# The MLPs of a two-layer hybrid block, multiplied by two by two blocks with seven products for eight

## The chip, the cores and the metric

One core of one Trainium2 chip runs the whole kernel. The metric is the device time of one execution in microseconds. Before the change it is 2652.65 us, the median of three runs (2652.08 to 2658.22). The engines are TensorE (PE; its weight loads, PEld, overlap with its matmuls), VectorE (DVE), ScalarE (ACT) and GpSimd (POOL); SyncE (SP) issues most transfers. The profile shows no transfer as an engine's work.

## The reference, cut to what matters

Two layers work on 512 latent tokens and 256 context tokens of width 1024. Each layer has token mixers and then an MLP; only the MLP changes. All is float32.

```
def sq_relu_mlp(h, w1, w2):                      # w1: 1024 x 4096, w2: 4096 x 1024
    return jnp.square(jax.nn.relu(h @ w1)) @ w2
...
    x = x + g1x * yx                              # yx: the token mixers' output
    hx2 = rmsnorm(x, g_mlp[i]) * (1.0 + sc2x) + sh2x
    x = x + g2x * sq_relu_mlp(hx2, w_ff1[i], w_ff2[i])
    if need_ctx:                                  # layer 0 alone
        ctx = ctx + g1c * yc
        hc2 = rmsnorm(ctx, g_mlp[i]) * (1.0 + sc2c) + sh2c
        ctx = ctx + g2c * sq_relu_mlp(hc2, w_ff1[i], w_ff2[i])
```

So the MLP of layer 0 has 768 token columns and that of layer 1 has 512.

## The kernel before

Activations lie transposed, features on partitions and tokens along the free dimension, as eight tiles x[k] of 128 rows. A float32 matrix product is made of three matmuls: each operand is split into a high half (rounded to float32r) and a low half (the rest), and high by high, high by low and low by high are summed in PSUM (`mm_T`, L438). One output tile is a call of `T_tile` (L451): eight weight blocks of 128 x 128, three matmuls each, per segment of at most 512 token columns.

Weights come in pages of 128 x 1024 floats (512 KB) by the class `Stream` (L220 to L273): a load on SP's queue, a high half on POOL or ACT (L246, L244), a low half on DVE (L257). It runs a page ahead. Their order is recorded in a first dry pass over the program.

The MLP (from L1644) goes by four chunks of 1024 inner features. For each chunk, eight tiles of the first matrix (`ff1`): ACT applies relu from PSUM (L1661), POOL squares (L1662), ACT and DVE split the result (L391, L392). Then eight tiles of the second matrix, which DVE multiplies by a gate and adds into x (L1686). The inner layer stays in SBUF. Layer 0's last chunk is split by token groups (L1693 to L1708), so that the next layer's norm can begin early.

Ahead of the MLP the output projection (tile wo) works in two halves of the columns, `grp`, and the norm of each half (`norm_tail`: multiply by the reciprocal root on DVE or POOL, shift on POOL at L531, split) runs as a background generator while PE works on other tiles; the first five ff1 tiles take the first half alone while the norm of the second is made. Background generators advance by one step per `tick()`; `mods_gen` computes the next layer's modulation vectors on DVE during layer 0's MLP (L371, L373).

SBUF pages of 128 x 768 floats come from one pool of 46 (`pg`), PSUM from four banks of one size (`aps`) and two double ones (`dps`). Every engine and queue works in the order of the program.

Of the kernel before, what the change touches and what calls it, by code (L numbers as in the profile page):

```python
# [12 lines left out]
F32 = mybir.dt.float32  # L13
# [8 lines left out]
LAT = 512  # L22
# [14 lines left out]
NPG = 46  # L37
NRAW = 2
PE_COLS = tuple(range(8, 16))
# [104 lines left out]
def kernel(ctx: ExitStack, tc: tile.TileContext, A: dict, order: list, record: bool, tap=None):  # L144
# [37 lines left out]
    SQ1 = None  # L182
    ALT = ("AD", "PD")
    WOR = 1
    FFR = 1
# [34 lines left out]
    class Stream:  # L220
# [5 lines left out]
        def load(self, j):  # L226
            while self.nraw <= j and self.nraw < len(order):
                k = order[self.nraw]
                a, b = _page_shape(k)
                t = wp.tile([128, 1024], F32, tag="wr", bufs=NRAW, name=nm("wr"))[:, :a * b]  # L230
                nc.sync.dma_start(t, A["wst"][woff[k]:woff[k] + 128 * a * b].rearrange("(p n) -> p n", p=128))
                self.raw[self.nraw] = t
                self.nraw += 1

        def split(self, j):
            while self.nsp <= j and self.nsp < len(order):
                self.load(self.nsp)
                t = self.raw.pop(self.nsp)
# [21 lines left out]
        def get(self, key):  # L260
            if record:
                order.append(key)
            assert order[self.nget] == key, (order[self.nget], key)
            self.split(self.nget)
            if self.nsp == self.nget + 1:
                self.flush()
            self.nget += 1
            return self.hl.pop(self.nget - 1)

        def ahead(self):  # L270
# [41 lines left out]
    junk_a = cst.tile([128, 96], BF16, name="junk_a")  # L312
    rope = cst.tile([128, 2, 4, 32], F32, name="rope")
    vec = [cst.tile([128, NV], F32, name=f"vec{i}") for i in range(depth)]
# [4 lines left out]
    o_d = [drp.tile([8, 128, TOK], F32, name=f"o_d{i}") for i in range(depth)]  # L319
    x_d = drp.tile([8, 128, LAT], F32, name="x_d")  # L320

    def spread_c(streams=(0, 1)):
# [237 lines left out]
    def proj_tok(keys_, hi, lo, toks, N):  # L560
# [8 lines left out]
        for key in keys_:  # L569
            wh, wl = W.get(key)  # L570
            nk = _page_shape(key)[0]
            for k in range(nk):
# [11 lines left out]
                tick()  # L584
        return ds_

    def norm_tail(nr, g, w0, wait, gap, engines):
# [333 lines left out]
    for k in range(6, KT):  # L921
        load_cols(k)
    nc.sync.dma_start(rope, A["rope"])
    for i in range(depth):
# [23 lines left out]
    for i in range(depth):  # L948
# [17 lines left out]
        def small_gen():  # L966
            dve.scalar_tensor_tensor(out=gna, in0=vc[:, V_NAQ:V_NAQ + 1], scalar=0.125, in1=vc[:, V_NAK:V_NAK + 1],
                                     op0=ALU.mult, op1=ALU.mult)
            dve.scalar_tensor_tensor(out=gml, in0=vc[:, V_MQN:V_MQN + 1], scalar=1.0 / math.sqrt(96.0),
                                     in1=vc[:, V_MKN:V_MKN + 1], op0=ALU.mult, op1=ALU.mult)  # L970
            for w in range(2):
                t = rg[w]
# [650 lines left out]
        grp = (((0, 0, 256),), ((0, 256, 512),)) if last else even  # L1623
        nrm2 = Norm(i, x, V_GMLP, 32, 24, grp)
        nf = None
        for g, parts in enumerate(grp):
            a, b = parts[0][1], parts[-1][2]
            W.mode = WOM[g]
            bg.rate = WOR
            for m in range(8):  # L1630
                ps = T_tile(("o", i, m), yh, yl, ((a, b),), "wo")
                for s, p0, p1 in parts:
                    dve.scalar_tensor_tensor(out=x[m][:, p0:p1], in0=ps[:, p0 - a:p1 - a], scalar=g1h[:, s, m:m + 1],
                                             in1=x[m][:, p0:p1], op0=ALU.mult, op1=ALU.add)
                nrm2.stat(m, g, SQ0 if g else None)
            if g == 0:
                nf = bg.add(norm_tail(nrm2, 0, *(TL0, TL4)[i]), front=True)
        bg.finish(nf)
# [4 lines left out]

        mark(f"L{i} mlp")  # L1644
        W.defer = DF[5]
        nf = bg.add(norm_tail(nrm2, 1, *(TL1, TL5)[i]), front=True)
# [175 lines left out]
```

## Time and profile before

| what | value |
|---|---|
| median of three runs | 2652.65 us |
| profiled execution | 2651.59 us |
| its span, first to last instruction | 2649.8 us |
| PE, PEld busy | 2486.3 us (94%), 2194.4 us (83%) |
| DVE, ACT, POOL busy | 1614.6 us (61%), 797.6 us (30%), 895.8 us (34%) |
| granted TensorE clock, mean | 0.972 |
| moved to and from HBM | 255.33 MB read, 25.17 MB written |

Busy shares are means over the span. Matmuls are pipelined, so that one matmul's shown length is longer than the step from its start to the next one's; steps are read from a timeline. [...]

### The profile page before, as it was taken

How to read it: one execution, taken by the hardware profiler on the slowest of the kernel's cores; microseconds unless marked ns; L12 is line 12 of the kernel's file. 1: busy time of each engine (PE TensorE's matmuls, PEld its weight loads, DVE VectorE, ACT ScalarE, POOL GpSimd, SP SyncE). 2: the span in 40 equal slices, each digit the busy share in tenths (PEclk: the TensorE clock that was granted, in tenths of full speed). 3: DMA queues.
4: the chain of work that ended last, by engine and by line, in shares of the span. 5: the costliest groups of instructions: out<-in, count | busy, mean ns of one | idle time of the engine just before them, and what ended most of it. 6: DMA issues, size and time to landing. Idle time of an engine off the chain costs nothing.

```text
span 2649.8 us, 38124 instructions
## 1 busy us (share of the span) xinstructions
PE 2486.3 (94%) x14406; PEld 2194.4 (83%) x14406; DVE 1614.6 (61%) x3303; ACT 797.6 (30%) x1945; POOL 895.8 (34%) x822
## 2 busy tenths in 40 slices
PE   6978999999899998999999989899998898899999
PEld 6868889898788898888888877789887787788887
DVE  7878665775785575655452467565655876643343
ACT  2261241425682122010101125433325741201100
POOL 5232122243342355222222352222253534633222
PEclk6999999999899999999999999999999999899999
DMA  6234322332014433334431322322221045333332
GB/s 222 80 108 157 122 91 88 114 115 83 7 57 167 144 112 110 127 110 145 153 139 61 120 96 80 111 98 78 86 95 55 1 154 166 120 118 95 96 96 96
DMA packets 93255, 282.97 MB, mean 107 GB/s; under 512 B 11152, under 2 KB 11920, under 8 KB 93072
## 3 DMA queue, kind: packets, MB, share of 16 engines
q1 hardware_dynamic: 84240, 257.46, 28.9%
q10 hardware_dynamic: 6912, 15.73, 1.6%
q0 software_dynamic: 1920, 7.34, 0.7%
q8 instruction: 114, 1.87, 0.3%
q14 instruction: 69, 0.57, 0.1%
HBM read 255.33 MB, written 25.17 MB: 106 GB/s over the span
## 4 chain that ended last, share of the span: by engine, by line
PE 65%; DVE 19%; ACT 6%; issue 5%; POOL 4%; DMA 1%; SPq 0%; ACTq 0%; DVEq 0%; POOLq 0%
PE f L438 32%; PE gt L1111 7%; PE S L745 4%; PE pt L576 4%; PE pt L577 4%; PE pt L578 4%; DVE wl L257 3%; PE pv L794 3%; PE T L771 2%; PE br L438 2%; PE wo L438 2%; DVE u L1019 1%; DVE junk L371 1%; ACT junk_a L1408 1%; POOL xn L531 1%
## 5 line engine op out<-in xcount | busy, mean ns | idle before, releaser
L246 POOL TENSOR_SCALAR wh<-wr 128x1024 fp32r<-128x1024 f32 (+2 forms) x297 | 335.9, 1133 | 635.8 <-DMA wr<-wst 244.0
L257 DVE TENSOR_TENSOR wl<-wr,wh 128x1024 fp32r<-128x1024 f32 (+1 forms) x286 | 391.2, 1369 | 151.3 <-POOL wh L246 113.3
L438 PE MATMUL f<-h,wh 128*128 128x512 f32 (+2 forms) x808 | 282.8, 350 | 9.8 <-ACT rl L1661 9.1
L438 PE MATMUL f<-l,wh 128*128 128x512 f32 (+2 forms) x808 | 282.3, 349 | 3.2 <-DVE l L392 3.2
L438 PE MATMUL f<-h,wl 128*128 128x512 f32 (+2 forms) x808 | 280.3, 347 | 0.7 <-DVE wl L257 0.7
L438 PE MATMUL f<-uh,wh 128*128 128x512 f32 (+1 forms) x768 | 273.8, 356 | 5.2 <-DVE x L1700 3.5
L438 PE MATMUL f<-ul,wh 128*128 128x512 f32 (+1 forms) x768 | 273.3, 356 | 0.0
L438 PE MATMUL f<-uh,wl 128*128 128x512 f32 (+1 forms) x768 | 272.1, 354 | 0.0
L631 POOL TENSOR_SCALAR P<-P,rl 128x768 f32<-128x768 f32 (+2 forms) x160 | 136.9, 856 | 384.3 <-DVE rl L630 274.8
L1111 PE MATMUL gt<-h,wh 128*128 128x512 f32 (+1 forms) x576 | 220.0, 382 | 6.8 <-POOL wh L246 5.9
L392 DVE TENSOR_TENSOR ul<-rl,uh 128x768 fp32r<-128x768 f32 (+3 forms) x74 | 66.6, 899 | 255.0 <-ACT uh L391 255.0
L577 PE MATMUL pt<-wl,h 128*128 128x256 f32 (+2 forms) x720 | 211.4, 294 | 10.0 <-DVE wl L257 10.0
L1661 ACT ACTIVATE rl<-f 128x768 f32<-128x768 f32 (+3 forms) x74 | 46.7, 632 | 573.7 <-PE f L438 573.7
L576 PE MATMUL pt<-wh,h 128*128 128x256 f32 (+2 forms) x720 | 214.1, 297 | 5.4 <-POOL wh L246 3.3
L1111 PE MATMUL gt<-h,wl 128*128 128x512 f32 (+1 forms) x576 | 207.7, 361 | 8.8 <-DVE wl L257 8.8
L578 PE MATMUL pt<-wh,l 128*128 128x256 f32 (+2 forms) x720 | 211.0, 293 | 0.0
L1111 PE MATMUL gt<-l,wh 128*128 128x512 f32 (+1 forms) x576 | 208.1, 361 | 0.0
L1662 POOL TENSOR_TENSOR rl<-rl 128x768 f32<-128x768 f32 (+3 forms) x74 | 85.8, 1159 | 315.2 <-ACT rl L1661 315.2
L402 DVE TENSOR_TENSOR ptl<-T,pth 128x384 fp32r<-128x384 f32 (+2 forms) x288 | 132.2, 490 | 97.8 <-ACT pth L396 96.3
L438 PEld LDWEIGHTS f<-h,wh 128*128 128x128 f32 x808 | 155.0, 192 | 29.7 <-issue 5.6
L438 PEld LDWEIGHTS f<-l,wh 128*128 128x128 f32 x808 | 154.8, 192 | 21.5 <-DVE l L392 4.4
L438 PEld LDWEIGHTS f<-h,wl 128*128 128x128 f32 x808 | 154.3, 191 | 18.7 <-DVE wl L257 1.1
(279 smaller groups left out, 6235.3 us busy)
## 6 DMA issues: line engine op xcount, KB each, us to landing
wr<-wst SPq DMA_DIRECT2D x298, 512.0 KB, 3.5
mod<-wmod SPq DMA_DIRECT2D x108, 384.0 KB, 4.3
bias<-bias SPq DMA_DIRECT2D x32, 320.0 KB, 3.6
th_d<-th ACTq DMA_DIRECT2D x24, 384.0 KB, 2.4
thr<-th_d SPq DMA_DIRECT2D x24, 384.0 KB, 3.5
x<-x SPq DMA_DIRECT2D x16, 384.0 KB, 4.9
th_d<-th ACTq DMA_DIRECT2D x24, 256.0 KB, 2.0
thr<-th_d SPq DMA_DIRECT2D x24, 256.0 KB, 3.8
```

Source lines behind the costliest of these rows:

```text
L246: pool.tensor_scalar(hi, t, 1.0, 0.0, op0=ALU.mult, op1=ALU.add)
L257: eng.tensor_tensor(out=lo, in0=t, in1=hi, op=ALU.subtract)
L402: dve.tensor_tensor(out=lo, in0=ps, in1=hi, op=ALU.subtract)
L438: pe.matmul(ps[:, c:c + b - a], wt[:, k, :], mv[k][:, a:b], start=k == 0 and wt is wh and mv is hi, stop=k == kts - 1 and wt is wl)
L576: pe.matmul(o, hi[kk][:, c], wh[:, k, :], start=kk == 0, stop=False)
L577: pe.matmul(o, hi[kk][:, c], wl[:, k, :], start=False, stop=False)
L578: pe.matmul(o, lo[kk][:, c], wh[:, k, :], start=False, stop=kk == total - 1)
L631: pool.tensor_scalar(self.P[:, :w], self.P[:, :w], rl, 1.0, op0=ALU.mult, op1=ALU.mult)
L745: pe.matmul(S[:, c:c + ww], a[r0:r1, qc], b[r0:r1, k0:k0 + ww], start=i_ == 0, stop=i_ == 2)
L794: pe.matmul(o[:, a:b], v_block(V, t, h), mv, start=i_ == 0, stop=i_ == len(ops) - 1, skip_group_check=True)
L1111: pe.matmul(ps[:, :b - a], wt[:, k, :], mv[k][:, a:b], start=k == 0 and wt is wh and mv is hi, stop=k == KT - 1 and wt is wl)
L1662: pool.tensor_tensor(out=t[:, a:b], in0=t[:, a:b], in1=t[:, a:b], op=ALU.mult)
```

## The change

The whole MLP of layer 1, and that of layer 0 but for the second matrix of its last chunk (the plain part), is made by two by two blocks with seven products. A pair `p` is two weight pages, which hold a 2 x 2 arrangement of 512-row by 128-column blocks; the tokens fall in two halves of n columns, 384 in layer 0 and 256 in layer 1. Sums of weight blocks (s1 to s4) and of activation blocks ("1" to "4") are formed ahead; seven products of four k blocks and three matmuls each (84 matmuls a pair) land in three PSUM banks, and sums of these give the four output blocks. There are 16 pairs of the first matrix, all of them first; their outputs, relu and square done, go to DRAM (`u_d`), as three pages X, Y, Z that hold six of the blocks and differences of blocks. Then 12 (layer 0) or 16 (layer 1) pairs of the second matrix read them back, each block once for four pairs, and split them.

`BlockWeights` has its own loads, into three raw buffers in place of two, and its splits run five products ahead. `block_tail` takes the place of `norm_tail` and makes the combined activation blocks. The weight stream of the rest of the kernel is emptied before and after (`bar`). The table of rotary angles moves from a fixed tile to a load in each layer.

```
+    BLEAD = (5, 5)
+    BAHEAD = 5
+    BLOAD, BSPLIT = 6, 3
...
+                for q in (6, 5, 7, 3, 4) if p < BLEAD[i] else (1, 3, 6, 5, 7, 2, 4):
+                    if q != 3:
+                        seq.append((p, q))
+                    elif prev is not None:
+                        seq.append((prev, 3))
...
+    BLOCKS = {1: ("w11", "11"), 2: ("w12", "21"), 3: ("s4", "22"), 4: ("w22", "4"), 5: ("s1", "1"), 6: ("s2", "2"), 7: ("s3", "3")}
...
+        def sums(self, j):
+            if j < len(self.seq) and self.seq[j][1] == 6:
+                p = self.seq[j][0]
+                w11, w21, w22 = self.half(p, 0, 0), self.half(p, 1, 0), self.half(p, 1, 1)
+                pool.tensor_tensor(out=w11, in0=w11, in1=w21, op=ALU.subtract)
+                s2 = self.f[p, "s2"] = pg("s2")[:, :512]
+                pool.tensor_tensor(out=s2, in0=w22, in1=w11, op=ALU.subtract)
+                pool.tensor_tensor(out=w21, in0=w21, in1=w22, op=ALU.add)
+        def split(self, j):
...
+            if q == 6:
+                s4 = self.f[p, "s4"] = pg("s4")[:, :512]
+                pool.tensor_tensor(out=s4, in0=self.half(p, 0, 1), in1=src, op=ALU.subtract)
+            t = self.t[p, name] = wp.tile([128, 1024], F32R, tag="wh", bufs=8, name=nm(name))
+            split_block(t, 512, src)
...
+    def split_block(t, n, src, eng=dve):
+        act.activation(t[:, :n], src, AF.Copy)
+        eng.tensor_tensor(out=t[:, n:2 * n], in0=src, in1=t[:, :n], op=ALU.subtract)
+    def block_tail(nr, g, O, hf, n, w0, wait, gap, engines):
...
+                for eng, o, p, q in ((pool, b3, b22, b12), (dve, b12, b12, b11), (dve, b2, b22, b12), (pool, b21, b21, b2)):
+                    eng.tensor_tensor(out=o, in0=p, in1=q, op=ALU.subtract)
+                yield
+                for j, (name, src, eng) in enumerate((("2", b2, dve), ("1", b12, dve), ("3", b3, pool), ("4", b21, pool), ("22", b22, dve))):
+                    O[name][kk] = pg("h" + name, F32R)
+                    split_block(O[name][kk], n, src, eng)
...
+            dmul = lambda t: pool.tensor_tensor(out=t, in0=t, in1=t, op=ALU.mult)
+            def square(j, t, relu=True):
+                if relu:
+                    later(j + 1, lambda: act.activation(t, t, AF.Relu))
+                later(j + 1, lambda: dmul(t))
+            def add(out, ps, t):
+                dve.tensor_tensor(out=out, in0=ps[:, :n], in1=t, op=ALU.add)
+            def store(p):
+                for slot, k in enumerate("XYZ"):
+                    if k in S[p]:
+                        act.dma_start(u_d[i][p, slot][:, :2 * n], S[p][k][:, :2 * n])
...
+                elif q == 3:
+                    X, Y = st["X"], st["Y"]
+                    add(Y[:, h0], st.pop("c"), Y[:, h0])
+                    square(j, Y[:, h0])
+                    def sums():
+                        Z = st["Z"] = pg("bz")
+                        for o, a, b in ((Z[:, h1], Y[:, h1], Y[:, h0]), (Y[:, h0], Y[:, h0], X[:, h0]), (Z[:, h0], Y[:, h1], Y[:, h0])):
+                            pool.tensor_tensor(out=o, in0=a, in1=b, op=ALU.subtract)
+                    if last or p < 12:
+                        later(j + 1, sums)
+                    later(j + 4, lambda: store(p))
...
+                elif q == 7:
+                    Y = st["Y"]
...
+                        act.activation(Y[:, h1], st["b"][:, :n], AF.Copy)
+                    add(Y[:, h1], st["c"], Y[:, h1])
+                    square(j, Y[:, h1])
...
+            def xadd(m, h, src):
+                for s, a, b in grp[h]:
+                    dve.scalar_tensor_tensor(out=x[m][:, a:b], in0=src[:, a - h * n:b - h * n], scalar=mods[i][:, s, 40 + m:41 + m],
+                                             in1=x[m][:, a:b], op0=ALU.mult, op1=ALU.add)
+            def evac2(j, p, q):
+                st = S.setdefault(p, {})
+                c, m = divmod(p - 16, 4)
+                if q == 1:
+                    st["X"], st["Y"] = pg("bx"), pg("by")
+                    act.activation(st["X"][:, :n], st["b"][:, :n], AF.Copy)
+                elif q == 2:
+                    add(st["X"][:, :n], st.pop("a"), st["X"][:, :n])
+                    xadd(m, 0, st["X"][:, :n])
+                elif q == 6:
+                    act.activation(st["X"][:, n:2 * n], st["b"][:, :n], AF.Copy)
+                elif q == 7:
+                    Y = st["Y"][:, :n]
+                    act.activation(Y, st["b"][:, :n], AF.Copy)
+                    add(Y, st["c"], Y)
+                    xadd(m + 4, 1, Y)
+                elif q == 4:
+                    xadd(m + 4, 0, st.pop("b"))
...
+                elif q == 3:
+                    X = st["X"][:, n:2 * n]
+                    add(X, st.pop("c"), X)
+                    xadd(m, 1, X)
...
+            def plain_split():
+                k = plain[1]
+                if k < 8:
+                    plain[1] += 1
+                    uh[k], ul[k] = pg("uh", F32R), pg("ul", F32R)
+                    t = uf.pop(k)[:, :nq]
+                    act.activation(uh[k][:, :nq], t, AF.Copy)
+                    (pool if k % 2 else dve).tensor_tensor(out=ul[k][:, :nq], in0=t, in1=uh[k][:, :nq], op=ALU.subtract)
+            for j, (p, q) in enumerate(seq):
+                for f in todo.pop(j, ()):
+                    f()
...
+                if not last and j == nlead + 5 * BLEAD[i] + 4:
+                    spread_c()
+                    mgen = mbg.add(mods_gen(i + 1))
+                    mbg.rate = 0.3
+                BW.ahead(j + BAHEAD)
+                for o, name in loads.get(j, ()):
+                    for nme in ("21", "2") if name == "4" else (name,):
+                        for k in range(4):
+                            if k % 2 == 0:
+                                t = pg("uf")
+                            v = t[:, n * (k % 2):n * (k % 2) + n]
+                            slot, h = U_AT[nme]
+                            nc.sync.dma_start(v, u_d[i][4 * (o - 1) + k, slot][:, n * h:n * h + n])
+                            uf.setdefault((o, name), []).append(v)
...
+                for o, name in splits.get(j, ()):
+                    vs = uf.pop((o, name))
+                    if name == "4":
+                        for k in range(4):
+                            pool.tensor_tensor(out=vs[k], in0=vs[k], in1=vs[4 + k], op=ALU.subtract)
+                    for k in range(4):
+                        O[o][name][k] = pg("u" + name, F32R)
+                        split_block(O[o][name][k], n, vs[k], pool)
...
+                for k in range(4):
+                    for i_, (w0, b0) in enumerate(((0, 0), (0, n), (512, 0))):
+                        pe.matmul(ps, wt[:, w0 + 128 * k:w0 + 128 * k + 128], B[k][:, b0:b0 + n],
+                                  start=fresh and k == 0 and i_ == 0, stop=k == 3 and i_ == 2, skip_group_check=True)
+                    if k % 2:
+                        tick()
+                (evac1 if p < 16 else evac2)(j, p, q)
```

## Rows read from the trace of the kernel before

**Rows 1.** The page's chain that ended last, share of the span by line.
```profile
PE f L438 32%; PE gt L1111 7%; PE S L745 4%; PE pt L576 4%; PE pt L577 4%; PE pt L578 4%; DVE wl L257 3%; PE pv L794 3%; PE T L771 2%; PE br L438 2%; PE wo L438 2%; DVE u L1019 1%; DVE junk L371 1%; ACT junk_a L1408 1%; POOL xn L531 1%
```
**Rows 2.** Busy times by stretch, MLPs of layer 0, then of layer 1.
```profile
core 0: us, PE busy (x) PEld busy (x) DVE busy (x) ACT busy (x) POOL busy (x), PEclk, DMA share, GB/s
981.70:1470.90 489.20, 479.09 (x2735) 424.14 (x2736) 245.83 (x486) 61.68 (x90) 137.05 (x119) 1.00 0.34 119
1134.90:1202.10 67.20, 67.20 (x386) 58.98 (x385) 38.04 (x86) 11.61 (x14) 17.38 (x14) 1.00 0.30 104
...
2283.00:2645.70 362.70, 355.66 (x1667) 298.88 (x1666) 151.05 (x167) 44.41 (x84) 121.75 (x113) 0.99 0.32 102
2384.40:2427.90 43.50, 43.50 (x193) 36.03 (x192) 15.84 (x16) 8.61 (x14) 14.44 (x14) 1.00 0.28 86
```
**Rows 3.** Timeline of PE, 959.7 to 966: start, length, engine, line, operation, tiles, form.
```profile
959.86 0.33 PE L438 MATMUL wo<-yh,wh 128*128 128x384 f32 x1
...
965.93 0.33 PE L438 MATMUL wo<-yh,wl 128*128 128x384 f32 x1
```
**Rows 4.** Timeline of PE in layer 1's MLP, 2287 to 2290.
```profile
2287.49 0.28 PE L438 MATMUL f<-l,wh 128*128 128x256 f32 x1
...
2289.89 0.28 PE L438 MATMUL f<-h,wh 128*128 128x256 f32 x1
```
**Rows 5.** POOL by line and form: count, busy us, mean ns, idle before.
```profile
L1586 POOL TENSOR_TENSOR y<-y,thr 128x512 f32<-128x512 f32 x8 | 10.2, 1294 | 13.4 <-DVE thr L1584 13.4
...
L477 POOL TENSOR_TENSOR sq<-sq,sq 128x256 f32<-128x256 f32 x9 | 6.7, 740 | 12.0 <-ACT sq L471 9.2 <-DMA wr<-wst 2.6
...
L257 POOL TENSOR_TENSOR wl<-wr,wh 128x384 fp32r<-128x384 f32 x4 | 4.1, 1028 | 0.3
```
**Rows 6.** Timeline of POOL, 1017 to 1024.
```profile
1017.49 0.83 POOL L1662 TENSOR_TENSOR rl<-rl 128x384 f32<-128x384 f32 x1
1018.29 1.05 POOL L246 TENSOR_SCALAR wh<-wr 128x1024 fp32r<-128x1024 f32 x1
...
1021.35 2.02 POOL L246 TENSOR_SCALAR wh<-wr 128x1024 fp32r<-128x1024 f32 x1
```
**Rows 7.** Timeline of POOL, 2318 to 2328.
```profile
2322.87 0.62 POOL L1662 TENSOR_TENSOR rl<-rl 128x256 f32<-128x256 f32 x1
```
**Rows 8.** DVE by line and form, as in rows 5.
```profile
L1633 DVE SCALAR_TENSOR_TENSOR x<-wo,g1h,x 128x256 f32<-128x256 f32 x24 | 11.4, 475 | 0.7 <-PE wo L438 0.7
...
L392 DVE TENSOR_TENSOR yl<-y,yh 128x512 fp32r<-128x512 f32 x8 | 5.5, 693 | 6.1 <-ACT yh L391 6.1
...
L1633 DVE SCALAR_TENSOR_TENSOR x<-wo,g1h,x 128x384 f32<-128x384 f32 x8 | 4.9, 612 | 4.2 <-PE wo L438 4.0
...
L1633 DVE SCALAR_TENSOR_TENSOR x<-wo,g1h,x 128x128 f32<-128x128 f32 x8 | 2.7, 341 | 1.4 <-PE wo L438 1.4
```
**Rows 9.** Three single lines of DVE: duration in ns as least/median/most, first and last start.
```profile
L371 DVE SCALAR_TENSOR_TENSOR junk<-mod,sB x132: 934/951/2596, 97.4 to 1379.7; 128x768 bf16<-128x768 f32 x132
...
L373 DVE SCALAR_TENSOR_TENSOR junk<-mod,sB x132: 424/425/2318, 98.4 to 1380.7; 128x256 bf16<-128x256 f32 x132
...
L1686 DVE SCALAR_TENSOR_TENSOR x<-f,mods,x x80: 473/749/751, 1076.3 to 2645.7; 128x512 f32<-128x512 f32 x56, 128x256 f32<-128x256 f32 x24
```
**Rows 10.** Timeline of DVE, 1020 to 1026, beside rows 6.
```profile
1020.61 1.84 DVE L257 TENSOR_TENSOR wl<-wr,wh 128x1024 fp32r<-128x1024 f32 x1
1022.38 1.39 DVE L392 TENSOR_TENSOR ul<-rl,uh 128x384 fp32r<-128x384 f32 x1
...
1025.46 0.54 DVE L392 TENSOR_TENSOR ul<-rl,uh 128x384 fp32r<-128x384 f32 x1
```
**Rows 11.** Timelines of DVE and of POOL, 188 to 196.
```profile
189.01 7.33 DVE L257 TENSOR_TENSOR wl<-wr,wh 128x1024 fp32r<-128x1024 f32 x1 [1.99 <-POOL wh L246]
...
189.95 5.31 POOL L1062 TENSOR_TENSOR rg<-rg,u 128x768 f32<-128x768 f32 x3
```
**Rows 12.** Busy times by stretch, the start of the kernel, columns as in rows 2.
```profile
0.00:30.00 30.00, 18.39 (x85) 17.02 (x85) 14.83 (x36) 11.27 (x16) 2.53 (x5) 0.73 0.93 348
...
30.00:60.00 30.00, 20.76 (x99) 18.57 (x99) 28.00 (x50) 4.76 (x6) 26.21 (x14) 0.61 0.39 142
```

More of the change, by code (lines that the diff above doesn't have):

```diff
@@ L268, in get, with bar @@
             return self.hl.pop(self.nget - 1)
+        def bar(self):
+            self.flush()
+            if record:
+                order.append(BAR)
+            assert order[self.nget] == BAR and self.nsp == self.nraw == self.nget
+            self.nget = self.nsp = self.nraw = self.nget + 1
         def ahead(self):
@@ L320 @@
     x_d = drp.tile([8, 128, LAT], F32, name="x_d")
+    u_d = [drp.tile([16, 3, 128, TOK], F32, name=f"u_d{i}") for i in range(depth)]
     def spread_c(streams=(0, 1)):
@@ L1624, with bkeys @@
         nrm2 = Norm(i, x, V_GMLP, 32, 24, grp)
+        if BLK[i]:
+            n = nq // 2
+            pairs = list(range(16 + 4 * (4 if last else 3)))
+            oset = lambda p: 0 if p < 16 else 1 + (p - 16) // 4
+            O = [{name: [None] * 4 for name in U_AT} for _ in range(5)]
+            hf = {}
+            def bkeys(p):
+                if p < 16:
+                    m = 8 * (p // 4) + p % 4
+                    return ("ff1", i, m), ("ff1", i, m + 4)
+                c, m = divmod(p - 16, 4)
+                return ("ff2", i, c, m), ("ff2", i, c, m + 4)
+            seq, prev = [], None
+            for p in range(BLEAD[i]):
+                seq += [(p, 1), (p - 1, 2)] if p else [(p, 1)]
+            seq.append((BLEAD[i] - 1, 2))
+            for p in pairs:
+                for q in (6, 5, 7, 3, 4) if p < BLEAD[i] else (1, 3, 6, 5, 7, 2, 4):
[3 more added lines that the diff above has]
+                        seq.append((prev, 3))
+                prev = p
+            seq.append((prev, 3))
         nf = None
@@ L1635 @@
                 nrm2.stat(m, g, SQ0 if g else None)
+                if BLK[i] and g and m >= 6:
+                    if m == 6:
+                        BW = BlockWeights(seq, [bkeys(p) for p in range(len(pairs))])
+                        BW.load()
+                    else:
+                        W.bar()
+                        BW.ahead(1)
             if g == 0:
-                nf = bg.add(norm_tail(nrm2, 0, *(TL0, TL4)[i]), front=True)
+                nf = bg.add(block_tail(nrm2, 0, O[0], hf, n, *TB0) if BLK[i] else norm_tail(nrm2, 0, *(TL0, TL4)[i]), front=True)
         bg.finish(nf)
```

214 lines of the change are left out of this document (211 added, 3 removed).

## The prediction

> **What bounds the kernel now.** I read the chain of waits first: the reader is to see that the MLP's matmuls (tile f) alone hold 32% of it, and that no other line comes near [rows 1]. Then the busy times by stretch: in layer 0 the MLP part that the change replaces runs from 981.7 to 1470.9 (489.2 us) and an inner chunk of eight tiles takes 67.2 us with PE busy throughout, DVE 38.0 and POOL 17.4; in layer 1 it runs from 2283.0 to 2645.7 (362.7 us), a chunk takes 43.5 us, DVE 15.8 and POOL 14.4 [rows 2]. So PE sets the pace, and everything else hides. A "pair" below is two such tiles, the unit of the change: 16.8 us in layer 0 (67.2/4), 10.88 in layer 1. What the parts before and after the chunks cost beyond that (981.7 to 1470.9 less 28 pairs: 18.8 us; layer 1, less 32 pairs: 14.4) is the norm's serial stretch; I leave it as it is.
>
> **PE's share of the change.** A pair becomes 7 products of 12 matmuls, 84, with 384 columns in layer 0 and 256 in layer 1. 384 columns follow one another every 0.1734 us (36 matmuls, 6.07 us over 35 steps) [rows 3], 256 every 0.120 (21 matmuls, 2.40 over 20) [rows 4]: 14.57 us a pair for 16.8, and 10.08 for 10.88. The second gain is small because a matmul of 256 columns takes more than half of one of 512 (43.5/192 = 0.227 us [rows 2]). Over 28 and 32 pairs PE saves 62.4 + 25.6 = 88 us. That is all the change can give.
>
> **What DVE and POOL get in its place.** Per pair, in the code of the change: POOL forms three weight sums and one more in the split (four operations of 512 columns with two different inputs, 1.294 us each [rows 5]); DVE makes seven low halves of 512 columns (0.693 [rows 8]); ACT makes the high halves. For the first product matrix POOL also squares four blocks and forms three differences for the stored page; for the second, POOL makes seven low halves of activations and one difference, and DVE adds into x, three times from SBUF. POOL with two inputs takes 1.028 us for 384 columns and 0.740 for 256 [rows 5]; squaring (one input twice) 0.83 and 0.62 [rows 6, 7]; DVE's add into x 0.475 for 256 columns, 0.612 for 384, 0.341 for 128 [rows 8].
> Layer 0, first matrix: POOL 5.18 + 3.32 + 3.08 = 11.58, DVE 4.85. Second: POOL 5.18 + 8 x 1.028 = 13.40, DVE 4.85 + 0.612 + 2 x (0.341 + 0.475) = 7.09.
> Layer 1, first: POOL 5.18 + 2.48 + 2.22 = 9.88, DVE 4.85. Second: POOL 5.18 + 5.92 = 11.10, DVE 4.85 + 3 x 0.475 = 6.28.
> Each engine by itself stays near PE's time. They are not by themselves. At 1020.61 DVE starts an operation with two SBUF inputs; POOL's next one, which takes 1.05 us when free, starts at 1021.35 and lasts 2.02, ending 0.92 us after DVE's end; DVE's next, 0.54 us when free, starts at 1022.38 and lasts 1.39, ending 0.40 after POOL's end [rows 6, 10]. Each waits for the whole of the other but for about 0.14 us. At 189.01 one DVE low half lasted 7.33 us behind three POOL operations in a row [rows 11]. DVE reading PSUM doesn't wait: 80 adds, 473 to 751 ns at the most, with POOL at work [rows 9]. So the two times add: 16.43 and 20.49 us a pair in layer 0, 14.73 and 17.38 in layer 1, each above its PE time, and all but the first above the pair of before.
> Layer 0: 16 x 16.43 - 4 x 3.08 (four pairs store no third page) + 12 x 20.49 = 496.5. The modulation vectors of the next layer run here as before, 66 steps of 0.951 + 0.425 us with two SBUF inputs [rows 9]: 90.8, hidden until now. The norm's second half now builds the combined blocks: for each of four k, two differences and two low halves on POOL (4 x 1.028), two differences and three low halves on DVE (5 x 0.54 [rows 10]), 4 x 6.81 = 27.2, less the 8 low halves of before (4.3): 22.9. The plain last chunk splits eight pages read back, on both engines in turn, an estimate of 12.6 from two operations of 384 each. Sum 622.8, and 18.8 of serial stretch: 641.6 against 489.2, +152.4.
> Layer 1: 16 x 14.73 + 16 x 17.38 = 513.8, the norm's extra 17.5 by the 256-column rows, 14.4: 545.7 against 362.7, +183.0.
> Together +335. Against it stands the 0.14 us at each hand-over. DVE's operations of this kind number 408 in layer 0 and 292 in layer 1; if each stands between two POOL operations, 700 x 0.28 = 196 us come back: +139. If they come in runs, as at 189, nearly nothing does. Both patterns stand in the trace; POOL's sums come in threes and its low halves in fours, DVE's splits one at a time, so I take half: **+237**.
>
> [...]
>
> **What else is added, and what hides it.** ACT: 7 high halves of 512 columns and 7 to 10 smaller copies a pair; before, it took 0.83 us for 768 columns (11.61/14) and 0.62 for 512 (8.61/14) [rows 2], so 14.1 and 10.5 us at the most, near PE's time and below the shared sum. Its stores wait for POOL's differences, and the high halves of later weights queue behind them; while POOL has work given to it earlier this costs nothing, and if not, up to one pair's lag at a time. The read-backs go through SP's queue behind weight loads that wait for one of three buffers; they are issued six products ahead, 12 us at the new pace. Traffic grows by about 69 MB (44 pages of 0.39 MB and 48 of 0.26 written, and 96 and 128 blocks of half a page read back, with 16 for the plain chunk); the thickest stretch, layer 1's second matrix, asks 34 MB in at least 174 us, 193 GB/s, where the start of the kernel moved 348 [rows 12]. The empty weight queue at each change of streams: 0 to 5 us, four times, under PE's last wo tiles; taken as nothing. The rope load per layer: nothing, one small load.
>
> **The sum.** The profiled execution took 2651.6 us, span 2649.8 and 1.8 around it; the runs' median is 2652.7, so the two agree. 2651.6 + 237 = 2889, forecast **2890 us**; full credit 2791, none 2987.
>
> **Rivals.**
> *No credit at all*, 2987: runs on POOL as at 189 keep DVE out each time. For it: the code gives POOL up to eight operations at once. Against: rows 6 and 10 show strict turns. 0.15.
> *The clock falls as well*, 3030. PE would idle 30% of the time. [...] Against: the grant was 1.00 and 0.99 over the MLPs of before, short idle times and all (10 and 7 us) [rows 2]. 0.15.
> *POOL alone counts*, 2616, faster: the waiting above belongs to those shapes, and 512-column halves pass beside POOL. Then layer 0 is PE's (-62.4), layer 1's first matrix too (-12.8), its second POOL's (+3.5), and POOL's part of the norm's extra and the plain chunk costs 36. It decides if DVE's low halves last under 0.8 us beside a busy POOL. Rows 6, 10 and 11 speak against it. 0.06.
> *PE stays the bound*, 2564, all 88 us. It needs the same, and the tails hidden. 0.03.
> *The round trip through DRAM or the pages run short*, over 3050: ACT's stores wait for POOL, pages come free late, and both engines idle together. Nothing in the rows gives a price but the lag of one pair (15 to 20 us) now and then; ten of them would do. 0.06.
> The forecast has the rest, 0.55.
>
> **Numbers.** The range runs from 2775 (just under full credit) to 3050 (the clock case inside); outside are the two fast cases and the last. Anything beyond 0.3% (8 us) can be told from no change here: faster 0.09, same 0.01, slower 0.90.
>
> **What would show it.** A chunk of four pairs of layer 1's first matrix lasting 50 to 60 us, not 40; DVE's 512-column low halves at 1.0 us or more in the mean against 0.693, POOL's sums over 1.5 against 1.294; PE's idle time ended by low halves and sums; POOL busy 90% in the MLP. The prediction is wrong if these operations keep their free durations with both engines busy, or if PE is gapless and a chunk takes 40 us (14.57 x 4 = 58 in layer 0).

## The result, and the profile after

The changed kernel takes **3048.99 us** (median of 4, 3047.27 to 3049.47) beside 2652.36 (2649.88 to 2658.22): ratio 1.149, interval 1.147 to 1.151. The forecast was 2890, the range 2775 to 3050; the direction came out, the size lies 1 us inside the upper end of the range.

The profiled execution took 3047.3 us, span 3045.5, 395.7 more than before. First the chain by line, the answer to [rows 1]:

```profile
PE 39%; DVE 21%; POOL 16%; issue 10%; ACT 8%; DMA 5%; SPq 0%; ACTq 0%; POOLq 0%; DVEq 0%
PE gt L1259 7%; PE S L891 4%; PE pt L595 3%; PE pt L596 3%; PE pt L597 3%; POOL u L682 3%; PE br L457 3%; PE pv L940 2%; POOL wr L648 2%; DVE wl L268 2%; PE fb L2011 2%; PE T L917 2%; POOL s L650 2%; DMA wr<-wst 2%; PE lu L457 2%
```

The MLP's matmuls, 32% of it before, are down to 2% for their largest group (fb, line 2011). PE's share fell from 65% to 39%, POOL's rose from 4% to 16%; its low halves of u and its weight sums (lines 682, 648, 650) are now among the named lines. The stretches, columns as in [rows 2] (PEclk, the granted clock, is a share of the full one; it stood at 0.50 from 2510.3 to 2543.3); of each layer the whole block part, its lead (the first four pairs' worth of products), and four pairs inside (28 products), twice for layer 1's first matrix; the last is one of layer 1's second matrix:

```profile
core 0: us, PE busy (x) PEld busy (x) DVE busy (x) ACT busy (x) POOL busy (x), PEclk, DMA share, GB/s
987.00:1654.20 667.20, 489.09 (x2399) 456.27 (x2400) 435.43 (x692) 222.61 (x450) 424.25 (x352) 0.86 0.41 145
987.00:1120.40 133.40, 75.69 (x350) 70.42 (x351) 58.65 (x87) 35.84 (x72) 79.71 (x77) 0.76 0.19 69
1205.60:1291.00 85.40, 69.47 (x337) 66.71 (x336) 59.02 (x99) 26.45 (x54) 51.40 (x44) 0.88 0.39 142
2480.30:3041.30 561.00, 400.79 (x2698) 377.96 (x2698) 273.33 (x429) 215.64 (x506) 394.94 (x397) 0.84 0.35 117
2480.30:2591.00 110.70, 58.02 (x346) 54.38 (x347) 47.12 (x86) 31.19 (x72) 63.69 (x69) 0.71 0.24 76
2591.00:2652.20 61.20, 46.17 (x339) 44.87 (x338) 28.23 (x44) 23.84 (x54) 47.70 (x48) 0.92 0.37 125
2652.20:2710.80 58.60, 46.79 (x339) 45.98 (x338) 27.34 (x40) 23.52 (x54) 43.17 (x44) 0.88 0.36 126
2845.00:2912.40 67.40, 50.82 (x338) 46.46 (x337) 36.54 (x57) 28.27 (x68) 49.67 (x49) 0.87 0.40 126
```

Layer 0's blocks take 667.2 us for 489.2, layer 1's 561.0 for 362.7: +178.0 and +198.3. The rest: 5.3 ahead of layer 0's blocks (987.0 for 981.7) and 14.0 between the two block parts (826.1 for 812.1, the plain chunk among them). Four inner pairs of layer 1's first matrix, 43.5 us before, take 61.2 and 58.6; and no engine is full in the second of these: PE 46.8, POOL 43.2, DVE 27.3. That alone doesn't tell a chain from engines that take turns, for POOL's and DVE's busy times, their waits inside, add up to 70.5. But the trace shows a chain. A lap of it, start, length, engine, operation and line:

```profile
2651.46 0.62 ACT s L681
2652.07 0.28 ACT bx L1891
...
2652.42 0.85 POOL bx L1842
2653.27 1.97 issue
2655.28 0.63 POOL by L1842
...
2655.97 1.08 POOL bz L1901
...
2657.12 1.07 POOL by L1901
...
2658.28 0.73 POOL bz L1901
2659.01 1.23 POOL wr L648
...
2660.32 1.27 POOL s L650
2661.61 0.34 ACT s L681
2661.98 0.45 ACTq L1856
2662.43 0.09 ACT by L1884
...
2662.57 2.94 PE fb L2011 x12
2665.53 0.42 DVE bx L1851
...
2666.30 0.61 ACT s L681
```

The last row is the first again, 14.84 us later (the next two laps take 15.53 and 14.85): one pair, one lap. A product ends, DVE adds it from PSUM, ACT takes the high half of a later weight and, behind it, a relu from PSUM (line 1891), POOL squares two blocks, forms the three differences of the stored page and only then, in the order of its queue, the sums of a weight block that is needed several products later. ACT's high half waits for that sum, and behind it in ACT's queue stand a store (line 1856) and the copy that frees the bank (line 1884), for which the array waits. So work for later products stands ahead of what the current one needs, in two queues. The waits from 2591 to 2774, three such stretches (engine and line, what it waited for, us, times, longest), name the same places:

```profile
ACT s L681 <- POOL s L650: 60.1, 12, 5.1
...
PE fb L2011 <- ACT by L1884: 35.0, 11, 4.3
```

The forecast had priced the two engines' shared access. It is in the trace too: the low halves of the weights on DVE, and two of POOL's sums (least, median and most in ns, first and last start):

```profile
L682 DVE TENSOR_TENSOR w<-wr,w x180: 676/692/1492, 986.9 to 3032.2; 128x512 fp32r<-128x512 f32 x180
L682 DVE TENSOR_TENSOR s<-s,s x120: 676/1076/1759, 1010.9 to 3033.7; 128x512 fp32r<-128x512 f32 x120
L682 DVE TENSOR_TENSOR s<-wr,s x120: 674/896/1773, 1014.6 to 3030.2; 128x512 fp32r<-128x512 f32 x120
...
L650 POOL TENSOR_TENSOR s<-wr,wr x60: 1261/1262/2033, 1008.9 to 3024.4; 128x512 f32<-128x512 f32 x60
...
L662 POOL TENSOR_TENSOR s<-wr,s x60: 1262/1730/1763, 1012.7 to 3026.8; 128x512 f32<-128x512 f32 x60
...
L1851 DVE TENSOR_TENSOR by<-fc,by x92: 409/425/558, 1066.8 to 3037.4; 128x256 f32<-128x256 f32 x48, 128x384 f32<-128x384 f32 x44
```

Free, a low half takes 0.68 us; 130 of the 420 take over 1. The adds that read PSUM don't wait: 0.41 to 0.56 us at the most, by their two widths. So there were two theories for the experiments: **A**, the engines take turns and their work adds up; **B**, the closed chain through the queues.

### The profile page after: what moved, and what is told of

Its sections match the earlier page's. It is cut to its first block, busy times and chain, and to the rows that moved or that the text cites. A ratio compares the mean times of both kernels' runs of the same rounds, so it can differ in the third digit from the quotient of the medians.

```text
span 3045.5 us, 42328 instructions
## 1 busy us (share of the span) xinstructions
PE 2543.5 (84%) x15102; PEld 2305.8 (76%) x15102; DVE 1945.8 (64%) x3797; ACT 1131.0 (37%) x2731; POOL 1443.3 (47%) x1338
## 3 DMA queue, kind: packets, MB, share of 16 engines
q8 instruction: 119, 1.95, 0.3%
## 4 chain that ended last, share of the span: by engine, by line
PE 39%; DVE 21%; POOL 16%; issue 10%; ACT 8%; DMA 5%; SPq 0%; ACTq 0%; POOLq 0%; DVEq 0%
PE gt L1259 7%; PE S L891 4%; PE pt L595 3%; PE pt L596 3%; PE pt L597 3%; POOL u L682 3%; PE br L457 3%; PE pv L940 2%; POOL wr L648 2%; DVE wl L268 2%; PE fb L2011 2%; PE T L917 2%; POOL s L650 2%; DMA wr<-wst 2%; PE lu L457 2%
## 5 line engine op out<-in xcount | busy, mean ns | idle before, releaser
L257 POOL TENSOR_SCALAR wh<-wr 128x1024 fp32r<-128x1024 f32 (+4 forms) x169 | 181.5, 1078 | 364.0 <-PE pt L596 85.6
L268 DVE TENSOR_TENSOR wl<-wr,wh 128x1024 fp32r<-128x1024 f32 (+1 forms) x156 | 227.8, 1464 | 136.7 <-POOL wh L257 99.9
L2011 PE MATMUL fb<-h,w 128*128 128x384 f32 (+1 forms) x888 | 177.9, 368 | 91.5 <-ACT by L1884 60.5
L2011 PEld LDWEIGHTS fb<-h,w 128*128 128x128 f32 x888 | 166.7, 240 | 100.6 <-ACT by L1884 65.9
L2011 PE MATMUL fb<-h,s 128*128 128x384 f32 (+1 forms) x768 | 141.8, 335 | 98.0 <-ACT h L681 45.7
L2011 PE MATMUL fb<-u,w 128*128 128x256 f32 (+1 forms) x672 | 132.5, 363 | 95.6 <-ACT by L1925 92.1
L2011 PEld LDWEIGHTS fb<-h,s 128*128 128x128 f32 x768 | 125.5, 206 | 108.7 <-ACT h L681 47.9
L682 POOL TENSOR_TENSOR u<-uf,u 128x256 fp32r<-128x256 f32 (+1 forms) x196 | 204.2, 1076 | 0.1
L682 DVE TENSOR_TENSOR w<-wr,w 128x512 fp32r<-128x512 f32 x180 | 141.4, 801 | 66.8 <-ACT w L681 65.3
L390 DVE SCALAR_TENSOR_TENSOR junk<-mod,sB 128x768 bf16<-128x768 f32 x132 | 157.8, 1196 | 23.0 <-DMA mod<-wmod 22.3
```

The source lines that it names most:

```text
L257: pool.tensor_scalar(hi, t, 1.0, 0.0, op0=ALU.mult, op1=ALU.add)
L268: eng.tensor_tensor(out=lo, in0=t, in1=hi, op=ALU.subtract)
L390: dve.scalar_tensor_tensor(out=junk, in0=t, scalar=1.0, in1=sB[s], op0=ALU.mult, op1=ALU.mult, accum_out=acc[:, s, j, 0:1])
L682: eng.tensor_tensor(out=t[:, n:2 * n], in0=src, in1=t[:, :n], op=ALU.subtract)
L2011: pe.matmul(ps, wt[:, w0 + 128 * k:w0 + 128 * k + 128], B[k][:, b0:b0 + n], start=fresh and k == 0 and i_ == 0, stop=k == 3 and i_ == 2, s ...
```

## The experiments

**One-input low halves.** DVE copies the high half into the place of the low one, so one of the two SBUF inputs goes.

```
-            split_block(t, 512, src)
+            act.activation(t[:, :512], src, AF.Copy)
+            dve.tensor_scalar(t[:, 512:1024], t[:, :512], 1.0, 0.0, op0=ALU.mult, op1=ALU.add)
```

> The seven low halves of a pair's weights on DVE read one SBUF input in place of two: the high half alone is copied to the low half's place, 512 columns, as many DVE operations as before (so the low parts of the weights are wrong). POOL, ACT, PE, the transfers and the order stay. Theory A (DVE operations with two SBUF inputs and POOL's operations exclude each other, and their sum is the pair's time): 4.85 us a pair leave the sum; layer 1's inner pairs go from 15.3 and 16.8 us to 10 to 11 and 12.5 to 13, layer 0's from 21 and 24 to 16 and 20: 230 to 290 us less, 2760 to 2820 us. Theory B (the pair's time is a closed loop through the queues: POOL's squares, differences and weight sums, ACT's split of a sum and the copy from PSUM behind it, a product, DVE's add, relu, and POOL again): the loop keeps its members and only POOL's waiting inside them goes, 1.3 to 2.6 us a pair: about 110 us less, 2920 to 2950 us.

2925.19 us, ratio 1.103 (1.101 to 1.105): 124 less, inside B's window and above A's. But A's premise was wrong: one input doesn't free this operation from the turns. DVE, then POOL, in the same microseconds:

```profile
2842.15 1.52 DVE L665 TENSOR_SCALAR w<-w 128x512 fp32r<-128x512 f32 x1
2843.59 2.96 DVE L665 TENSOR_SCALAR s<-s 128x512 fp32r<-128x512 f32 x2
...
2847.31 0.42 DVE L665 TENSOR_SCALAR s<-s 128x512 fp32r<-128x512 f32 x1
```

```profile
2842.02 1.35 POOL L650 TENSOR_TENSOR s<-wr,wr 128x512 f32<-128x512 f32 x1
2843.34 1.47 POOL L651 TENSOR_TENSOR wr<-wr 128x512 f32<-128x512 f32 x1
2844.78 1.48 POOL L662 TENSOR_TENSOR s<-wr,s 128x512 f32<-128x512 f32 x1
```

Alone the copy takes 0.42 us (2847.31); beside POOL it lasts 1.52, until the sum has ended and 0.30 beyond (2843.67 against 2843.37), and the next two end 0.29 beyond the third sum (2846.55 against 2846.26). In turns of 0.42 us in place of 0.69, A gives 1.9 us a pair or 115 less, as near to 124 as B's 110; so this run doesn't tell the two apart.

**Differences two products later.** Order alone: the differences and the stores move behind later weights' sums.

```
-                        later(j + 1, sums)
-                    later(j + 4, lambda: store(p))
+                        later(j + 3, sums)
+                    later(j + 6, lambda: store(p))
```

> The three differences for the stored page are put into the program two products later, behind the next pair's three weight sums on POOL, and the stores two products later with them. Same operations, same shared time. Theory A: no change, 3035 to 3065 us. Theory B: three operations, 2.9 us, leave the loop of each pair of the first matrix: 28 pairs x 1.5 to 2.9 us = 40 to 80 us less, 2970 to 3010 us.

3020.86, ratio 1.139 (1.138 to 1.141): 28 less, between the two windows: more than A gives and less than B expected.

**Weights first.** The weights' preparation is issued ahead of the delayed squares and differences, one product earlier.

```
-    BAHEAD = 5
+    BAHEAD = 6
...
             for j, (p, q) in enumerate(seq):
+                BW.ahead(j + BAHEAD)
                 for f in todo.pop(j, ()):
...
-                BW.ahead(j + BAHEAD)
```

> The weight sums and splits run six products ahead in place of five and stand before the squares and differences of the same step in the program. Same operations, same shared time. Theory A: no change, 3035 to 3065 us. Theory B: the square and the three differences of a pair leave the way to the next pair's sums, and the second matrix gets one product more of lead: 60 to 120 us less, 2930 to 2990 us.

2977.43, ratio 1.123 (1.121 to 1.124): 72 less with not one operation fewer, inside B's window; A alone gives nothing here. The edit changes the order in the queues and starts the preparation a product earlier, and no run parts the two.

**Squares on ACT.** All squares of the first matrix leave POOL, 2.48 us a pair in layer 1.

```
-            dmul = lambda t: pool.tensor_tensor(out=t, in0=t, in1=t, op=ALU.mult)
+            dmul = lambda t: act.activation(t, t, AF.Square)
```

> The four squares of a pair of the first matrix go from POOL to ACT (its Square, in place, behind the relu). Theory A: 3.32 us a pair leave the sum in layer 0 and 2.48 in layer 1, 16 pairs each: 93 us less, 2945 to 2970 us. Theory B: POOL no longer waits for ACT's relu before the weight sums, and two squares, 1.5 us, and two hand-overs of some 0.3 us go out of the loop; ACT gets 1.7 to 2.1 us a pair, beside: 50 to 110 us less, 2940 to 3000 us. It does not tell the two apart by its time; by them the first matrix's chunks in layer 1 go from 61 us to 51 or to 53 to 57.

3055.82, ratio 1.153 (1.151 to 1.154): 7 more, where both theories expected less. Four pairs of layer 1's first matrix in this run:

```profile
2655.80:2718.80 63.00, 47.85 (x337) 45.41 (x337) 27.20 (x40) 31.30 (x74) 33.15 (x28) 0.91 0.34 117
```

POOL fell from 43.2 to 33.2 us and the stretch grew by 4.4. This refutes A as the whole account: the sum of the two engines' work went down and the time did not. Nor did B's windows, for time or stretch, come out. The chain of this run says why: the squares only changed the queue they stand in. Its lap, 15.7 us (2655.73 to 2671.41), runs through ACT (relu, square, high halves) and back to POOL's differences and sums, and over these four pairs and the four before POOL waits 57.2 us for ACT's squares.

**Both of the first and third edit together.**

> The two edits that each took time away, together: the low halves of the weights by a one-input copy on DVE (the low parts of these weights are wrong in this run; it shows time only) and the weights' preparation issued ahead of a product's delayed work instead of behind it. Alone they were worth 124 us (2925) and 72 us (2977). If they shorten different things (the load on the two engines' shared access, and the order in the queues), they add: 2835 to 2870. If both only shorten one closed chain of waits, the second finds the chain already cut by the first and something else late: 2890 to 2925. Below 2830 neither picture would hold.

2853.38, ratio 1.075 (1.073 to 1.077): 195.6 less, for 124 + 72 = 196. They add, so neither edit takes the other's gain, as the expectation asked of two separate costs.

**Three weight sums left out.**

```
-                pool.tensor_tensor(out=w11, in0=w11, in1=w21, op=ALU.subtract)
-                s2 = self.f[p, "s2"] = pg("s2")[:, :512]
-                pool.tensor_tensor(out=s2, in0=w22, in1=w11, op=ALU.subtract)
-                pool.tensor_tensor(out=w21, in0=w21, in1=w22, op=ALU.add)
+                self.f[p, "s2"] = w22
```

> Three of the four weight sums per pair left out on POOL (one raw block stands in for the third; the output is wrong, it shows time only). They take about 0.9 to 1.36 us each in the changed kernel's trace, some 3.2 us per pair, 60 pairs: 190 us of POOL's time. Shared access sets the time (theory A): the whole of it comes off, and somewhat more where DVE no longer waits, 2810 to 2870. Closed chain (theory B), in which only two of the three sums stand between a store and the next weights: 60 x 2 us = 120, 2900 to 2950. If neither sets the time but the half-clock stretches of the array do: within 30 us of 3049.

2865.52, ratio 1.080 (1.078 to 1.083): 183 less. The three take 3 x 1.27 = 3.8 us a pair, 229 over 60 pairs: 80% of POOL's time for them stood in the end time, 3.1 us a pair. Both theories have them on the path. The size lies in A's window, which was priced from 190 us; from 229, 183 is 46 short of all three, and from B's two sums, 152, it is 31 more. It decides little.

**Weights first, and the four sums on DVE.** The edit of weights first, and:

```
-                pool.tensor_tensor(out=w11, in0=w11, in1=w21, op=ALU.subtract)
+                dve.tensor_tensor(out=w11, in0=w11, in1=w21, op=ALU.subtract)
...
-                pool.tensor_tensor(out=s2, in0=w22, in1=w11, op=ALU.subtract)
-                pool.tensor_tensor(out=w21, in0=w21, in1=w22, op=ALU.add)
+                dve.tensor_tensor(out=s2, in0=w22, in1=w11, op=ALU.subtract)
+                dve.tensor_tensor(out=w21, in0=w21, in1=w22, op=ALU.add)
...
-                pool.tensor_tensor(out=s4, in0=self.half(p, 0, 1), in1=src, op=ALU.subtract)
+                dve.tensor_tensor(out=s4, in0=self.half(p, 0, 1), in1=src, op=ALU.subtract)
```

> Weights' preparation ahead of the delayed work (worth 72 us alone, 2977), and in addition the four weight sums on DVE instead of POOL; everything is still computed. By shared access (A) the sums go on excluding POOL's two-input work wherever they run; on DVE one takes 0.69 us alone against 1.29 on POOL, so 4 x 0.6 = 2.4 us per pair less, 60 pairs: 144 us below 2977, 2815 to 2860. By the chain alone (B) the sums leave POOL's queue, where they stood behind squares and differences, but come behind the adds and low halves in DVE's: 2860 to 2930. If a queue of DVE then sets the time (its adds free the array's banks): above 2960.

2871.88, ratio 1.083 (1.080 to 1.086): 106 less than with the order alone, 177 less than the change: inside B's window and 12 above A's. Of the versions that change both layers and leave nothing out it is the fastest, and still 8% behind the kernel before.

**Filler for the array.** Four repeated matmuls ahead of each fresh bank.

```
+                if fresh:
+                    for k in range(4):
+                        pe.matmul(ps, wt[:, 0:128], B[k][:, :n], start=True, stop=True, skip_group_check=True)
```

> Four repeated matmuls ahead of the first matmul of each fresh bank (their result is overwritten by the start flag; nothing else changes): 12 more per pair, 12 x 0.173 = 2.1 us in layer 0 and 12 x 0.120 = 1.4 us in layer 1, over 60 pairs 105 us of array time at full clock, 200 at half. If the array set the time: 3130 to 3200. If its time lies inside the gaps that the waits leave (A and B): 3040 to 3090, nearer the upper end by B, since a fresh bank's product is one link of the chain. If what costs is the half clock after idle stretches, and the filler keeps the clock up: 2980 to 3035.

3057.27, ratio 1.152 (1.150 to 1.154): 8 more for 105 us of array time. Two stretches of four pairs in layer 1's first matrix:

```profile
2600.80:2661.20 60.40, 50.55 (x386) 49.40 (x386) 28.09 (x43) 23.12 (x52) 47.23 (x47) 0.94 0.38 127
2661.20:2720.80 59.60, 49.34 (x386) 47.92 (x385) 27.87 (x40) 24.57 (x57) 43.85 (x44) 0.97 0.36 125
```

The granted clock is 0.94 and 0.97, for 0.92 and 0.88 in the same two stretches of the change, and their sum stayed: 120.0 us for 119.8. Neither the array's work nor its clock sets the time there.

**Low halves computed twice**, 420 two-input operations of 0.68 us more, **and in their place a maximum** of one SBUF input and the same length.

```
-            split_block(t, 512, src)
+            act.activation(t[:, :512], src, AF.Copy)
+            dve.tensor_tensor(out=t[:, 512:1024], in0=src, in1=t[:, :512], op=ALU.subtract)
+            dve.tensor_tensor(out=t[:, 512:1024], in0=src, in1=t[:, :512], op=ALU.subtract)
```

```
-            split_block(t, 512, src)
+            act.activation(t[:, :512], src, AF.Copy)
+            dve.reduce_max(t[:, 512:513], src, axis=AX)
+            dve.tensor_tensor(out=t[:, 512:1024], in0=src, in1=t[:, :512], op=ALU.subtract)
```

> The low half of every weight block is computed twice (same inputs, same place): 420 more two-input operations on DVE that read SBUF, 0.68 us each when POOL is idle, 287 us in all. Its pair is the next run, in which the added operation lasts as long but reads one operand. Shared access (A): DVE and POOL take turns, so what is added comes off POOL's time too: +200 to +290, 3250 to 3340. Closed chain (B): only the low halves that are links of it count, some 2 to 4 of 7 products: +80 to +160, 3130 to 3210, and the same in the next run.

> Instead of the second low half, a maximum over the 512 columns of the raw weight block on DVE (its result is overwritten): 420 operations with one SBUF input. In the trace of before such maxima took 418 ns for 256 columns and 950 for 768, so about 0.68 us, the same 287 us of DVE's queue as in the run before. Shared access (A): it needs no turn with POOL, and DVE has a third of its time idle: +0 to +100, 3050 to 3150, and at least 100 us below the run before. Closed chain (B): within 30 us of the run before.

3304.18 (1.246, 1.244 to 1.248) and 3146.14 (1.186, 1.184 to 1.188): +255 and +97 for the same 287 us on DVE, both inside A's windows; B alone wanted them within 30 us of each other. The maxima never waited for POOL:

```profile
L665 DVE TENSOR_REDUCE w<-wr x180: 668/677/687, 988.1 to 3133.3; 128x1 fp32r<-128x512 f32 x180
L665 DVE TENSOR_REDUCE s<-s x120: 669/680/687, 1016.5 to 3135.6; 128x1 fp32r<-128x512 f32 x120
```

All 420 stay between 668 and 687 ns, where the low halves reach 1773. But the pair tells the theories apart less than was expected: the maximum needs only the raw block, so it runs while DVE would have waited for ACT's high half (0.62 us), and the second low half can't. Part of the 158 us between them is that cover, and the two runs don't say how much.

**No additions.** One-input low halves, weights first, three weight sums out, and besides the differences of the stored page and the one of the blocks read back left out.

```
-                        Z = st["Z"] = pg("bz")
-                        for o, a, b in ((Z[:, h1], Y[:, h1], Y[:, h0]), (Y[:, h0], Y[:, h0], X[:, h0]), (Z[:, h0], Y[:, h1], Y[:, h0])):
-                            pool.tensor_tensor(out=o, in0=a, in1=b, op=ALU.subtract)
+                        st["Z"] = Y
...
-                    if name == "4":
-                        for k in range(4):
-                            pool.tensor_tensor(out=vs[k], in0=vs[k], in1=vs[4 + k], op=ALU.subtract)
```

> What the seven products would give if most additions were free: low halves by a one-input copy, weights' preparation first, three of four weight sums, the three differences of the inner blocks and the difference of the input blocks of the second product all left out (the output is wrong, it shows time only). From the runs so far: 2853 with the first two, and the sums were worth 183 by themselves, so 2670; the differences are 3 x 0.9 to 1.2 us in 28 pairs, 60 to 90 us of POOL, of which half or less should still count: 2610 to 2680 if the additions are what eats the gain. If leads and half clock keep it up: 2690 to 2760. The array alone would give 2564 and some 20 for what changed elsewhere.

2712.96, ratio 1.023 (1.022 to 1.025), inside the second window, the one for leads and a lower clock. Four inner pairs of each layer's first matrix, then the two leads:

```profile
1149.70:1208.00 58.30, 58.30 (x339) 58.30 (x338) 40.94 (x96) 28.52 (x56) 20.56 (x20) 1.00 0.60 214
2385.90:2426.30 40.40, 40.40 (x339) 40.40 (x339) 20.10 (x45) 25.08 (x55) 15.99 (x22) 1.00 0.57 202
988.20:1086.40 98.20, 66.94 (x350) 62.70 (x351) 46.77 (x89) 36.45 (x74) 49.87 (x56) 0.84 0.28 95
2311.40:2385.90 74.50, 50.72 (x346) 47.93 (x347) 39.24 (x88) 31.76 (x74) 36.35 (x47) 0.79 0.35 108
```

With the additions gone the array runs without a gap: 58.3 and 40.4 us for four pairs, 14.57 and 10.1 a pair. What stays above the array's time are the leads, which with 98.2 + 74.5 cost 74 more than it, and the second matrix, in which POOL still makes the low halves of the blocks read back: four pairs take 48 to 53 us in layer 1 for the array's 40.3, and 68 to 75 in layer 0 for 58.3.

**Layer 0 alone.**

```
-    BLK = (True, True)
+    BLK = (True, False)
```

> Only layer 0's MLP by seven block products, layer 1's as before. By the two traces layer 0's blocks took 667 against 489 us and what lies ahead of them 5 more, so 2652 + 178 + 5 to 25 = 2835 to 2860 if the layers are independent; below 2820 if the second layer's blocks cost more than their own 198 us by what they do to the stretch between the two MLPs.

2854.28, ratio 1.076 (1.075 to 1.078): +202, inside its window. 202 here leaves 195 for layer 1, near the trace's 198.3 for its blocks: the layers add.

**What the two theories leave.** For four inner pairs of layer 1's first matrix, the mean of two stretches (products 28 to 84 of the layer, by the starts of their first matmuls), beside what A adds up from the forecast's free durations (14.73 a pair; one-input halves 0.42 each):

```
run                          measured   sum of both engines
the change                     59.9       58.9
one-input low halves           54.9       51.3
differences later              56.1       58.9
weights first                  56.7       58.9
squares on ACT                 63.3       49.0
both                           50.3       51.3
three sums out                 45.7       43.4
weights first, sums on DVE     47.6       49.3
low halves twice               79.6       78.3
a maximum beside them          63.9       58.9
no additions (array: 40.3)     40.3       below the array
```

In the order of the change the measured time lies above the sum, by 1 to 5 us, and with the squares on ACT 14 above: there the lap through the queues is longer than the turns. Where later weights stand ahead of the differences (four rows) it lies 1 to 3 us under the sum, as two engines in turn would give, with the small overlap at each hand-over (0.22 us at a fourth weight sum) coming back. But that closeness doesn't show that turns alone set these rows. With weights first the chain closes again, by another way:

```profile
2581.07 0.75 POOL bz L1901
...
2581.84 1.11 ACTq L1856
...
2583.00 0.16 ACT by L1847
...
2583.33 0.61 ACT w L681
...
2583.97 0.70 DVE w L682
...
2584.73 3.37 DMA wr<-wst
...
2588.27 1.29 POOL wr L648
...
2595.54 0.75 POOL bz L1901
```

In this lap of 14.47 us, the store and a relu on ACT wait for POOL's last difference (bz), then come the high and the low half of a raw weight, the load of a later raw page (3.37 us), and only then POOL's next sums, squares and differences. The laps of the run with both edits (12.5 to 12.6 us) and of the one with the sums on DVE (11.5 to 11.7) also go through such a load, and four of them make the 50.3 and 46.7 us that four pairs take there. No run gives the loads another buffer or an earlier start, so what this lap costs isn't shown.

So the change pays for turns and for its lap. That its own time comes out near the sum doesn't show that the sum alone sets it; how the two share a given microsecond the runs don't settle.

## Why the prediction was right, and where it was off

That 3049 lies inside the range is luck in part: the upper end stood at 3050 to hold a fall of the clock, and where a run raised the clock (0.94 and 0.97 for 0.92 and 0.88), nothing was gained.

**PE's share: right.** 14.57 and 10.08 us a pair were forecast, 58.3/4 = 14.57 and 40.4/4 = 10.1 measured once nothing else was in the way. The 88 us exist; no run here reached them.

**The added two times: a real cost, and a total that came out partly by luck.** After the leads the sum without credit is 521.5 us in layer 0 (12 x 16.43 - 4 x 3.08 + 12 x 20.49 + 90.8) and 454.8 in layer 1 (12 x 14.73 + 16 x 17.38), 976 together. Measured: 667.2 - 133.4 = 533.8 and 561.0 - 110.7 = 450.3, 984. In layer 1 the total hides two misses: the first matrix's part (2591.0 to 2774.4) took 183.4 us for 176.8, the second's (to 3041.3) 266.9 for 278.1. And with the squares on ACT the sum fell and the time did not. So the two engines' work costs time, but its sum doesn't set the time by itself.

**The credit for hand-overs: the step that failed.** Half of 196 us was to come back, some 85 of it after the leads; by 984 against 976 nothing did. The overlap is real (a fourth weight sum takes 1.73 us where the free sum and low half make 1.27 + 0.68 = 1.95), and in layer 1's second matrix 11 us came back; but a chain through the engines' queues spent more than that elsewhere. The forecast had the parts of that chain, ACT's stores and high halves that wait for POOL, and priced them at nothing while POOL "has work given to it earlier". It has: but its queue goes in order (in the lap, squares and differences from 2652.42, the sum only at 2659.01), and the work given earlier is the wrong work. Weights first gives back 72 us of what that clause left out.

**The leads: mis-sized.** They were taken as four pairs and the norm: 65.7 + 22.9 + 18.8 = 107.4 and 58.9 + 17.5 + 14.4 = 90.8, 198 in all without credit; they took 133.4 + 110.7 = 244. They shrink to 105.7 and 88.1 with weights first and one-input halves together, 50 of the 145 us by which they exceed the array's time for four pairs (58.3 + 40.4): a third of that goes with the same two edits. What holds the rest was not tried by itself.

**The small terms.** The plain chunk: 12.6 forecast, 14.0 for all between the block parts. The emptied weight queue, taken as nothing of 0 to 5 a time: 5.3 before layer 0. Missing credit 93 (984 - 891), leads 59 above their own half-credit share (244 - 185), 5.3 and 1.4: 159, which is the 158 between 2889 and 3047.3. (Layer 1's serial stretch of 14.4 is 14.5 by its own numbers; it changes nothing.)

**The signs it named.** The chunk of 50 to 60 us came out at its upper edge, 58.6 and 61.2. The others did not: low halves 0.90 us in the mean over the 420, not 1.0; three of the four sums at their free 1.26 to 1.29 in the median, not over 1.5; POOL busy 43.2 of 58.6 us, 74%, not 90; PE's idle time ended by ACT's copy, line 1884. Together they already hinted that turns are not all of it.

**The rivals.** POOL alone and PE alone fell by the pattern of [rows 6, 10, 11], seen again above. No credit at all (2987) has the right sum but no place for leads and queue. The clock's 3030 stands 140 us above the forecast, a term that no run shows. The clock did fall, from 1.00 and 0.99 [rows 2] to 0.86 and 0.84, but it set no time in the stretch tried: with the filler it was higher and nothing was gained. The case beyond 3050, round trips and both engines idle together, is the nearest in kind to what happened, though no run tries the round trip itself.

## What to carry to other kernels

A saved matmul is bought with additions, and here these went to two engines that wait for each other: before counting the array's gain, add up POOL's work and every DVE operation whose rows show it waiting for POOL (here subtractions of two SBUF inputs, 0.68 us and up to 1.77, and one-input copies, 0.42 and up to 1.52, not maxima, 0.67 to 0.69, and not adds from PSUM, 0.41 to 0.56), and count no overlap until the order is known. Then follow the queues, each in its order: what a later product needs should be issued so early that it neither waits behind the current product's delayed work nor holds up what frees the current bank. Where the engines aren't full and durations are near their free ones, look in the chain for a lap that repeats; its time is the price, and when one lap is shortened another can take over, as the load did with weights first.

## What the runs showed of the hardware that was not expected

A copy on DVE with one SBUF input waited for POOL like a subtraction with two (0.42 us alone, 1.52 beside a sum), while a maximum over the same 512 columns never did (668 to 687 ns, 420 times) and neither did adds that read PSUM (409 to 558 ns, 200 times). With four repeated matmuls ahead of every fresh bank the granted clock was 0.94 and 0.97, for 0.92 and 0.88, in two stretches that together took the same time.
